# Score products of attention and retention: the product of the low parts over all 128 rows instead of 64

## Chip, cores and metric

The kernel runs on one core of a Trainium2 chip. The metric is the device time of one execution in microseconds (us); the figure for the kernel before is the median of 3 runs.

## What is computed

Four blocks act one after the other on 512 tokens of 1024 channels: twice block 1 (three mixers and a gated feed-forward), twice block 2 (attention, a linear recurrence and a gated MLP). The change touches the scores in two of these parts:

```
# block 1, retention, 4 heads, 64 lanes of q and k per head (written out over all pairs of tokens)
scores = einsum('bhncd,bhnmd->bhncm', qc, kc) * decay        # q, k rotated
# block 2, attention, 8 heads, 128 lanes without and 64 with rotation
q = concatenate([q_nope, q_rope], -1); k = concatenate([k_nope, k_rope], -1)
s = einsum('bqhd,bkhd->bhqk', q, k) * scale
p = softmax(where(mask, s, -1e30))
```

All is float32. The kernel gets there with float32r products (the faster form of TensorE): every operand is split into a high and a low part that sum to it, and a product is hi·hi + hi·lo + lo·hi; the product of the two low parts is left out (`mm3`, lines 319 to 324).

## The kernel before

**Layout.** One program, no loops on the chip: Python writes out some 37,000 instructions, and each engine runs its own in the order in which the program was written. `Stream` (line 147) brings the weights: pieces of 128 x 2048 columns by DMA on the queue of SyncE (SP, line 166), each half ("chunk", 128 x 1024) split into `whi` by ScalarE (line 179) and `wlo` by VectorE (line 180), some four to six chunks ahead of TensorE. `projT` (line 330) multiplies 128 columns of weights with an operand over all 512 tokens: 3 matmuls for each 128 rows, so a chunk is 24 matmuls of 512 columns. There are 8 PSUM buffers, given out in turn.

**Retention** (block 1). After the rotation of q and k, `stack` (line 537) builds for each head, by DMAs between SBUF tiles, `qs` = (q1 hi, q2 hi, q1 lo, q2 lo), 32 lanes each, `ks` = (k1 hi, k2 hi, k1 hi, k2 hi), and `kl` = (k1 lo, k2 lo), the latter in rows 0 to 63 alone (lines 728 to 731). The DMAs of a stack alternate between the queues of GpSimd and SyncE. In `ret_head` (line 609) the scores of 128 keys are two matmuls: line 620 over all 128 rows (hi·hi and hi·lo at once), line 621 over 64 rows (`kl` with the high parts of q). VectorE multiplies them by the decay (line 623). The four heads run in two lanes that step forward between the weight products, so line 620 and line 621 come in groups of two heads: 4 pairs of matmuls, a pause of weight products, 4 pairs again.

**Attention** (block 2, `mla`, line 947). For each head: `scores(h)` (line 986) is, for each of four blocks of 128 queries, five matmuls into one PSUM buffer: lines 997 to 999 the 128 lanes without rotation (q hi·k hi, q hi·k lo, q lo·k hi), line 1000 the rotated lanes (q as hi and lo stacked to 128 rows, the high parts of k held twice), line 1001 the rotated lanes with the low parts of k, over rows 0 to 63. The low parts of k are there in rows 64 to 127 as well (`mla_down` writes the rotated lanes twice). VectorE takes the row maximum (line 1003), ScalarE the exponential (line 1005), VectorE scales (line 1015). Meanwhile TensorE runs the projections of the next head, whose split (lines 314 and 315) ends on VectorE, and what `FILL` lists for this head (products with values, weight products of z_b, the rotated queries of heads 4 to 7 after the scores of head 2). Then `out(h)` (line 1018) transposes the probabilities (line 1026), and the scores of the next head follow.

Of the kernel before, what the change touches and what calls it, by code (L numbers as in the profile page):

```python
# [15 lines left out]
S = 512  # L16
# [12 lines left out]
# column offsets of w_in, block 1  # L29
# [3 lines left out]
# column offsets of w_in, block 2  # L33
# [7 lines left out]
# columns of the per-channel table  # L41
# [16 lines left out]
# rows that are broadcast over the partitions  # L58
# [10 lines left out]
def lru_outside(m):  # L69
    """The channels outside tile m that the gates of tile m depend on: (tile, first, last + 1)."""  # L70
    b0, b1 = (128 * m) // LBW * LBW, ((128 * m + 127) // LBW + 1) * LBW
    out = []
    if b0 < 128 * m:
        out.append((m - 1, b0 - 128 * (m - 1), 128))
    if b1 > 128 * m + 128:
        out.append((m + 1, 0, b1 - 128 * (m + 1)))
    return out
# [7 lines left out]
# the tiles of the recurrence whose gates come with a tile of z_c  # L85
ZPOS = (4, 6, 7, 8)
# what follows the scores of each head: v values, g rotated queries of the second group, p the product
# with the values of the head before, z a z_b
# [44 lines left out]
class Tl:  # L133
    """A tile of 2 KiB per partition, and the slot that it sits in."""
# [12 lines left out]
class Stream:  # L147
    """The weights, in the order in which they are used: pieces of 128 rows, 1024 columns to
    a chunk, two chunks to a DMA; each chunk is split into two float32r parts that sum to it."""
# [19 lines left out]
    def _split(self, c):  # L169
        nc = self.k.nc  # L170
        p = c // 2
        while self.loaded <= p:
            self._load(self.loaded)
            self.loaded += 1
        raw = self.raw[p]
        src = raw[:, 1024 * (c % 2):1024 * (c % 2) + 1024]
        hi = self.k.wp.tile([128, 1024], F32R, tag="whi", name=f"whi{c}")
        lo = self.k.wp.tile([128, 1024], F32R, tag="wlo", name=f"wlo{c}")
        nc.scalar.activation(hi[:], src, AF.Copy)  # L179
        nc.vector.tensor_tensor(lo[:], src, hi[:].bitcast(F32), op=ALU.subtract)  # L180
        self.parts[c] = (hi, lo)
        self.parts.pop(c - RING, None)
        # the next pair is asked for as soon as this one's last half is read
        if c % 2 == 1 and self.total is not None:
            if self.loaded < (self.total + 1) // 2 and self.loaded <= p + RAW:
                self._load(self.loaded)
                self.loaded += 1
# [15 lines left out]
    def take(self, n, spec):  # L203
        """The next n columns of the stream, in two parts."""
        n //= 64
        if self.fill + n > UNITS:
            while self.fill < UNITS:
                self.order.append(None)
                self.fill += 1
            c = self.next()  # L210
            self.fill = 0
            self.cur = c
            if self.total is None:
                self.parts[c] = (Mock(), Mock())
            else:
                assert c <= (self.floor if self.floor is not None else c) + RING - 1
                self.ahead(c if self.lazy else c + AHEAD)
                assert self.split > c
        o = self.fill
        self.order.append((n, spec))  # L220
        for _ in range(n - 1):
            self.order.append(0)
        self.fill += n
        hi, lo = self.parts[self.cur]
        return hi[:, 64 * o:64 * (o + n)], lo[:, 64 * o:64 * (o + n)]
# [5 lines left out]
class Op:  # L231
    """An operand of the tensor engine with features on partitions, in two float32r parts."""
# [5 lines left out]
class Kernel:  # L238
# [64 lines left out]
    def split(self, t, n=512, eng=None):  # L303
        """The two parts of an SBUF tile, which is freed."""
        hi, lo = self.s.t(F32R), self.s.t(F32R)
        self.nc.scalar.activation(hi[:, :n], t[:, :n], AF.Copy)  # L306
        (eng or self.nc.vector).tensor_tensor(lo[:, :n], t[:, :n], hi[:, :n].bitcast(F32), op=ALU.subtract)  # L307
        self.s.f(t)
        return Op(hi, lo)

    def split_ps(self, ps):
        """The two parts of a PSUM tile, which is freed."""
        hi, lo = self.s.t(F32R), self.s.t(F32R)
        self.nc.scalar.activation(hi[:], ps[:], AF.Copy)
        self.nc.vector.tensor_tensor(lo[:], ps[:], hi[:].bitcast(F32), op=ALU.subtract)
        self.p.f(ps)
        return Op(hi, lo)

    def mm3(self, ps, a, b, first, last):
        """ps += a^T b for operands in two parts (the product of the low parts is below float32)."""  # L320
        mm = self.nc.tensor.matmul
        mm(ps, a[0], b[0], start=first, stop=False)  # L322
        mm(ps, a[0], b[1], start=False, stop=False)  # L323
        mm(ps, a[1], b[0], start=False, stop=last)  # L324

# [4 lines left out]
    def projT(self, name, l, cols, op=None, ps=None):  # L330
        """128 columns of a weight matrix times an operand, tokens along the free axis."""
        key = (name, l, cols)
        if key in self.pre:
            return self.pre.pop(key)
        op = op or self.h_op
        bl = self.blocks(name, l, len(op), cols)
        ps = self.p.t()
        for k, w in enumerate(bl):
            self.mm3(ps[:], w, (op[k].hi[:, :], op[k].lo[:, :]), k == 0, k == len(op) - 1)
        return ps  # L340

    def projT_halves(self, specs):
        """The first columns after a norm: the first half of the tokens while the norm of the second
        half is still under way."""
        pend, self.pend = self.pend, None
        ws = self.ws
# [6 lines left out]
        n = len(specs)  # L353
# [32 lines left out]
    def pre_norm(self, tb, g, spill):  # L386
        """h = rmsnorm(x) of a token block."""
        nc = self.nc
        sq = self.small(4, "sq")
        x = [self.x[tb, hf] for hf in range(2)]  # L390
        h = [self.s.t() for hf in range(2)]
# [16 lines left out]
    def transposes(self, tb):  # L408
        """h of a token block to features on partitions, split."""
# [13 lines left out]
    def post_norm(self, tb, ps, g):  # L423
        """x += rmsnorm(y) of a token block, y in PSUM."""
# [19 lines left out]
    def out_proj(self, name, l, nk, get, done, g_post, g_pre, spill, last=False, head=4, tail=4):  # L444
        """y = op @ W with tokens on the partitions, then the norms of each token block as it is done.
        get(k): operand k. done(k): it isn't needed any more."""
# [66 lines left out]
    def norm_tail(self, gn, spill):  # L513
        """What is left of the norms when the next products start."""
        self.transposes(2)
        self.pre_norm(3, gn, spill)
        self.s.f(*gn)
        yield
        self.transposes(3)
        yield  # L520

# [1 line left out]
    def rotate(self, a, b, cos, sin):  # L523
        """The rotated halves of four heads, split: a and b hold them in PSUM, and are freed."""
# [13 lines left out]
    def stack(self, h, parts):  # L538
        """A tile with 32 lanes of head h from each of the parts."""
# [32 lines left out]
    def cf_norm(self, l, c, out):  # L572
        """silu(layernorm(c)), split."""
# [35 lines left out]
    def ret_head(self, h, qs, ks, kl, v, sg, out):  # L609
# [5 lines left out]
        for j in range(NT):  # L615
# [5 lines left out]
            mm(ps[:, :S - n0], kl[h][0:64, js], qs[h][0:64, n0:], start=False, stop=True)  # L621
# [42 lines left out]
    def merge(self, l, wg, cg, wy, ops, acc, n_br, last):  # L664
        """acc (+)= sigmoid(gate) * (op @ W); the last branch gives the operands of the output product."""
# [33 lines left out]
    def tok_proj(self, name, l, cols, n, evac):  # L699
        """Token-major product of h with n columns."""  # L700
# [13 lines left out]
    def mixers1(self, l):  # L714
# [8 lines left out]
        def rope():  # L723
            for nm, a, b in (("q", qa, qb), ("k", ka, kb)):
# [4 lines left out]
                else:  # L729
                    rot["ks"] = [self.stack(h, (x1.hi, x2.hi, x1.hi, x2.hi)) for h in range(4)]  # L730
                    rot["kl"] = [self.stack(h, (x1.lo, x2.lo)) for h in range(4)]
# [71 lines left out]
    def ffn_half(self, l, ch):  # L803
        """A tile of the conv of the up-projection."""
# [53 lines left out]
    def mla_down(self, l):  # L858
        """c_q, c_kv (normed, split) and the rotated key lanes."""
# [20 lines left out]
        for tb in range(NT):  # L880
# [19 lines left out]
            # the rotated key lanes, twice  # L900
# [46 lines left out]
    def mla(self, l, c, zb):  # L947
        """Attention; zb[h] = silu(z_b) becomes y_b of head h."""
# [38 lines left out]
        def scores(h):  # L987
# [4 lines left out]
            for i in range(NT - 1, -1, -1):  # L992
# [8 lines left out]
                mm(ps[:, :nn], qr[0:64, ts], kr.lo[0:64, :nn], start=False, stop=True)  # L1001
# [15 lines left out]
        def out(h):  # L1017
            """The probabilities with keys on partitions: in two parts, those of the last 128 keys whole."""
# [42 lines left out]
        def z(h):  # L1061
            """z_b of a head, whose product may have come first."""
# [37 lines left out]
    def lru(self, l):  # L1100
# [4 lines left out]
        # -8 softplus(-lam), and twice that  # L1105
# [30 lines left out]
        def pack(m):  # L1136
            """The outside channels of tile m in one tile (high, low, high parts), or in one per part."""
# [14 lines left out]
        def gate_weights(m):  # L1152
            """The blocks of tile m, and those of its outside channels."""
# [99 lines left out]
    def gmlp(self, l):  # L1253
# [31 lines left out]
        def spatial(c):  # L1285
            """u * (ws v + bs) * silu(z): z in y."""
# [105 lines left out]
def order():  # L1392
    """The order in which the blocks of the weights are used."""
# [20 lines left out]
def _cols(name, cols):  # L1414
    """Columns of a weight matrix, as a slice or a list."""
# [11 lines left out]
def lay_out(inp):  # L1427
# [19 lines left out]
    def put(key, a):  # L1447
        """a: (taps, channels) -> columns tile by tile, taps inside."""
# [56 lines left out]
```

## Time and profile before

| what | value |
|---|---|
| median of 3 runs | 3267.53 us (3271.23, 3267.14, 3267.53) |
| profiled execution: its span, the only time that the page gives for it | 3272.1 us, 36878 instructions |
| TensorE busy with matmuls | 3216.5 us (98%) |
| TensorE busy with loads of weights | 2651.4 us (81%) |
| VectorE busy | 1871.1 us (57%) |
| ScalarE busy | 1193.4 us (36%) |
| GpSimd busy | 252.0 us (8%) |
| mean rate of the DMA | 103 GB/s |

Matmuls overlap: the busy time of one is longer than the distance from its start to the start of the next. That distance is what a matmul costs on TensorE, so starts are read, not durations. Idle time of an engine that bounds nothing costs nothing.

### The profile page before, as it was taken

The numbers are of one execution on the slowest core, as the hardware profiler recorded it, in microseconds if no ns is written. First come the engines' busy times: TensorE is split into PE (matmuls) and PEld (weight loads), VectorE is DVE, ScalarE is ACT, GpSimd is POOL, SyncE is SP. The second block draws the span as 40 slices with busy tenths as digits, with TensorE's granted clock in tenths as the row PEclk, the third lists the DMA queues.
The fourth block names the chain that finished last, engine by engine and source line by source line (L and its number), as shares of the span: only waits on it lengthen the run. The fifth ranks groups of instructions, "written<-read, shape, count | busy, mean of one in ns | idle before, by whom it ended". The sixth has DMA issues, their size and how long they took to land. (4 is left out here: it accounts for less than half of the span.)

```text
span 3272.1 us, 36878 instructions
## 1 busy us (share of the span) xinstructions
PE 3216.5 (98%) x14808; PEld 2651.4 (81%) x14808; DVE 1871.1 (57%) x2729; ACT 1193.4 (36%) x1798; POOL 252.0 (8%) x354
## 2 busy tenths in 40 slices
PE   8999999999999999999999999999999999999998
PEld 7888888888888888888887887788888788778887
DVE  5677556663667755666358536635445744653543
ACT  4222343342422234334245526522234543642222
POOL 2000010000200001000010002200001000220000
PEclk9999999999999999999999999999999999999999
DMA  5222322332422232233222124322333123333231
GB/s 191 90 92 90 129 88 93 106 113 103 145 84 94 90 129 88 93 107 112 103 103 80 63 95 129 117 103 93 113 116 118 64 77 103 115 117 109 90 103 71
DMA packets 61899, 336.93 MB, mean 103 GB/s; under 512 B 10048, under 2 KB 10176, under 8 KB 26912
## 3 DMA queue, kind: packets, MB, share of 16 engines
q1 hardware_dynamic: 49600, 302.02, 26.3%
q0 software_dynamic: 10976, 30.55, 3.1%
q8 instruction: 116, 1.90, 0.2%
q10 hardware_dynamic: 1152, 2.01, 0.2%
q14 instruction: 55, 0.45, 0.0%
HBM read 310.68 MB, written 8.39 MB: 98 GB/s over the span
## 5 line engine op out<-in xcount | busy, mean ns | idle before, releaser
L322 PE MATMUL p<-hh,whi 128*128 128x512 f32 (+1 forms) x2752 | 1052.4, 382 | 1.6 <-ACT whi L179 1.6
L324 PE MATMUL p<-hh,wlo 128*128 128x512 f32 (+1 forms) x2752 | 1046.7, 380 | 1.4 <-DVE wlo L180 1.4
L323 PE MATMUL p<-hl,whi 128*128 128x512 f32 (+1 forms) x2752 | 1046.8, 380 | 0.0
L180 DVE TENSOR_TENSOR wlo<-raw,whi 128x1024 fp32r<-128x1024 f32 x544 | 676.9, 1252 | 529.4 <-ACT whi L179 528.3
L179 ACT ACTIVATE whi<-raw 128x1024 fp32r<-128x1024 f32 x544 | 562.6, 1052 | 290.6 <-PE p L324 199.4
L322 PEld LDWEIGHTS p<-hh,whi 128*128 128x128 f32 x2752 | 519.9, 189 | 101.3 <-ACT whi L179 2.0
L324 PEld LDWEIGHTS p<-hh,wlo 128*128 128x128 f32 x2752 | 519.4, 189 | 100.7 <-DVE wlo L180 1.7
L323 PEld LDWEIGHTS p<-hl,whi 128*128 128x128 f32 x2752 | 520.0, 189 | 97.1
L322 PE MATMUL p<-s,whi 128*128 128x512 f32 (+1 forms) x768 | 306.8, 399 | 1.7 <-ACT s L306 1.7
L323 PE MATMUL p<-s,whi 128*128 128x512 f32 (+1 forms) x768 | 304.9, 397 | 1.8 <-POOL s L307 1.8
L324 PE MATMUL p<-s,wlo 128*128 128x512 f32 (+1 forms) x768 | 304.9, 397 | 0.0
L323 PE MATMUL p<-wlo,s 128*128 128x512 f32 x640 | 253.8, 397 | 0.0
L322 PE MATMUL p<-whi,s 128*128 128x512 f32 x640 | 253.5, 396 | 0.0
L324 PE MATMUL p<-whi,s 128*128 128x512 f32 x640 | 252.2, 394 | 0.0
L306 ACT ACTIVATE s<-s 128x512 fp32r<-128x512 f32 x168 | 103.2, 626 | 367.4 <-DVE s L688 133.6
L672 ACT ACTIVATE s<-p 128x512 f32<-128x512 f32 x96 | 57.3, 597 | 470.7 <-PE p L324 470.7
L812 DVE SCALAR_TENSOR_TENSOR s<-p,pv,s 128x511 f32<-128x511 f32 (+1 forms) x176 | 131.8, 749 | 122.3 <-ACT s L809 119.2
L683 DVE TENSOR_TENSOR s<-p,s 128x512 f32<-128x512 f32 x96 | 66.3, 691 | 204.0 <-PE p L324 203.9
L566 DVE SCALAR_TENSOR_TENSOR s<-s,pv,s 128x511 f32<-128x511 f32 (+14 forms) x240 | 176.1, 734 | 5.7
L322 PEld LDWEIGHTS p<-s,whi 128*128 128x128 f32 (+1 forms) x768 | 144.6, 188 | 37.5 <-ACT s L306 2.5
L323 PEld LDWEIGHTS p<-s,whi 128*128 128x128 f32 (+1 forms) x768 | 145.0, 189 | 36.6 <-POOL s L307 2.7
L324 PEld LDWEIGHTS p<-s,wlo 128*128 128x128 f32 (+1 forms) x768 | 144.9, 189 | 34.7
(187 smaller groups left out, 3094.3 us busy)
## 6 DMA issues: line engine op xcount, KB each, us to landing
raw<-in_w_dram SPq DMA_DIRECT2D x272, 1024.0 KB, 4.8
s<-in_rows_dram POOLq DMA_DIRECT2D x32, 256.0 KB, 3.5
xd<-s SPq DMA_DIRECT2D x24, 256.0 KB, 2.0
s<-xd POOLq DMA_DIRECT2D x24, 256.0 KB, 3.2
s<-s POOLq DMA_DIRECT2D x88, 64.0 KB, 2.5
s<-s SPq DMA_DIRECT2D x80, 64.0 KB, 2.7
s<-in_cst_dram POOLq DMA_DIRECT2D x16, 256.0 KB, 3.4
s<-in_x_dram POOLq DMA_DIRECT2D x8, 256.0 KB, 4.5
```

The costliest lines, as they stand in the source:

```text
L179: nc.scalar.activation(hi[:], src, AF.Copy)
L180: nc.vector.tensor_tensor(lo[:], src, hi[:].bitcast(F32), op=ALU.subtract)
L306: self.nc.scalar.activation(hi[:, :n], t[:, :n], AF.Copy)
L322: mm(ps, a[0], b[0], start=first, stop=False)
L323: mm(ps, a[0], b[1], start=False, stop=False)
L324: mm(ps, a[1], b[0], start=False, stop=last)
L566: nc.vector.scalar_tensor_tensor(c[:, sh:], glu[:, :S - sh], w(k), c[:, sh:], op0=ALU.mult, op1=ALU.add)
L672: nc.scalar.activation(sgs[m][:], pg[:], AF.Sigmoid)
L683: nc.vector.tensor_tensor(sg[:], py[:], sg[:], op=ALU.mult)
L812: nc.vector.scalar_tensor_tensor(t[:, sh:], ps[:, :S - sh], w(k), t[:, sh:], op0=ALU.mult, op1=ALU.add)
```

## The change

Three places, all in the scores. Line 1001 multiplies all 128 rows of `qr` with all 128 rows of `kr.lo`, line 621 all 128 rows of `kl` with all 128 rows of `qs`, so both now add the product of the low parts. For the latter, line 731 stacks the low parts of k twice, by four DMAs per head instead of two. The number of matmuls, their columns and their order stay. The rest of the diff drops comments and leaves the line numbers.

```diff
@@ ret_head
-            mm(ps[:, :S - n0], kl[h][0:64, js], qs[h][0:64, n0:], start=False, stop=True)
+            mm(ps[:, :S - n0], kl[h][:, js], qs[h][:, n0:], start=False, stop=True)
@@ mixers1, rope
-                    rot["kl"] = [self.stack(h, (x1.lo, x2.lo)) for h in range(4)]
+                    rot["kl"] = [self.stack(h, (x1.lo, x2.lo, x1.lo, x2.lo)) for h in range(4)]
@@ mla, scores
-                mm(ps[:, :nn], qr[0:64, ts], kr.lo[0:64, :nn], start=False, stop=True)
+                mm(ps[:, :nn], qr[:, ts], kr.lo[:, :nn], start=False, stop=True)
```

## Rows read from the trace of the kernel before

**Rows 1.** The page: busy time by engine, and granted clock in 40 slices.
```profile
PE 3216.5 (98%) x14808; PEld 2651.4 (81%) x14808; DVE 1871.1 (57%) x2729; ACT 1193.4 (36%) x1798; POOL 252.0 (8%) x354
PEclk9999999999999999999999999999999999999999
```
**Rows 2.** Groups of instructions by line and shape, TensorE: busy us and mean ns of one.
```profile
L997 PE MATMUL p<-s,s 128*128 128x256 f32 x32 | 12.3, 384 | 0.0
L1001 PE MATMUL p<-s,s 64*128 64x256 f32 x32 | 12.1, 380 | 0.0
...
L1000 PE MATMUL p<-s,s 128*128 128x256 f32 x32 | 8.9, 280 | 0.0
```
**Rows 3.** Timeline, TensorE, scores of head 1, first block 2: start us, duration us, line.
```profile
1747.55 0.40 PE L998 MATMUL p<-s,s 128*128 128x512 f32 x1
...
1748.01 0.40 PE L1000 MATMUL p<-s,s 128*128 128x512 f32 x1
1748.34 0.49 PE L1001 MATMUL p<-s,s 64*128 64x512 f32 x1
1748.76 0.44 PE L997 MATMUL p<-s,s 128*128 128x384 f32 x1
1749.04 0.34 PE L998 MATMUL p<-s,s 128*128 128x384 f32 x1
...
1750.25 0.28 PE L998 MATMUL p<-s,s 128*128 128x256 f32 x1
...
1750.49 0.28 PE L1000 MATMUL p<-s,s 128*128 128x256 f32 x1
...
1752.33 0.40 PE L323 MATMUL p<-s,whi 128*128 128x512 f32 x1
```
**Rows 4.** Timeline, loads of weights (PEld) in the same scores.
```profile
1747.78 0.19 PEld L1000 LDWEIGHTS p<-s,s 128*128 128x128 f32 x1
1748.34 0.18 PEld L1001 LDWEIGHTS p<-s,s 64*128 64x128 f32 x1 [0.37 <-issue]
```
**Rows 5.** Timeline, TensorE, recurrence of block 2: a matmul over 96 rows.
```profile
2003.46 0.39 PE L324 MATMUL p<-s,wlo 128*128 128x512 f32 x1
2003.69 0.39 PE L1170 MATMUL p<-s,whi 96*128 96x512 f32 x1
2003.92 0.39 PE L322 MATMUL p<-s,whi 128*128 128x512 f32 x1
```
**Rows 6.** Timeline, TensorE, retention: two groups of four pairs, each from its start to its end.
```profile
145.71 0.40 PE L620 MATMUL p<-s,s 128*128 128x512 f32 x1
...
149.16 0.40 PE L323 MATMUL p<-hl,whi 128*128 128x512 f32 x1
...
154.45 0.28 PE L620 MATMUL p<-s,s 128*128 128x256 f32 x1
...
157.18 0.40 PE L323 MATMUL p<-hl,whi 128*128 128x512 f32 x1
```
**Rows 7.** Timeline, VectorE and TensorE, from head 2 to the scores of head 4.
```profile
1771.21 0.69 DVE L529 TENSOR_TENSOR s<-p,s 128x512 f32<-128x512 f32 x1 [1.41 <-PE p L324]
...
1779.22 0.69 DVE L1003 TENSOR_REDUCE asm<-p 128x1 f32<-128x512 f32 x1
...
1784.38 1.28 DVE L315 TENSOR_TENSOR s<-p,s 128x512 fp32r<-128x512 f32 x2
...
1785.71 0.50 PE L998 MATMUL p<-s,s 128*128 128x512 f32 x1
```
**Rows 8.** Timeline, VectorE and TensorE, from head 1 to the scores of head 2.
```profile
1755.72 1.41 DVE L315 TENSOR_TENSOR s<-p,s 128x512 fp32r<-128x512 f32 x2
...
1758.74 0.39 PE L998 MATMUL p<-s,s 128*128 128x512 f32 x1
```
**Rows 9.** Timeline, queue of SyncE, ScalarE and VectorE, around the stacks of retention, first layer.
```profile
45.98 13.47 SPq L543 DMA_DIRECT2D s<-s  x20
...
67.34 1.06 ACT L179 ACTIVATE whi<-raw 128x1024 fp32r<-128x1024 f32 x1 [12.30 <-DMA raw<-in_w_dram]
...
80.62 0.69 DVE L553 TENSOR_TENSOR s<-p,s 128x512 f32<-128x512 f32 x1 [1.50 <-PE p L324]
```

## Prediction

> **What bounds the kernel now.** I read the page's busy times first: TensorE is busy for 3216.5 of 3272.1 us, VectorE for 57%, ScalarE for 36% [rows 1]. So TensorE's own sequence sets the time, and a change in it counts in full unless another engine comes into the way just there. The granted clock is full in every slice [rows 1], so nothing is to be had there. But busy is not the same as fast: matmuls overlap, and what one costs is the distance to the next start. So the second view is the groups by line and shape, for matmuls of equal size that differ in length. The products over 64 rows with 256 columns take 380 ns, those on line 1000, of the same columns over 128 rows, 280 ns; and line 997, which follows a product over 64 rows, takes 384 ns although it has 128 rows [rows 2]. Something is lost on either side of each 64-row product. The third view, the timeline of TensorE, tells how much.
>
> **What a 64-row product costs.** In an undisturbed sequence 512 columns take (1748.01 - 1747.55) / 2 = 0.23 us from start to start, and 256 columns (1750.49 - 1750.25) / 2 = 0.12 us [rows 3]; for 384 I take the middle, 0.172. Around line 1001 the starts are: line 1000 at 1748.01, line 1001 at 1748.34, line 997 at 1748.76, line 998 at 1749.04 [rows 3]. These are steps of 0.33, 0.42 and 0.28 us in place of 0.23, 0.23 and 0.172: 1.03 us instead of 0.63, so 0.40 us lost per 64-row product. The loads of weights show where: that of line 1000 starts at 1747.78, one matmul ahead of its use, that of line 1001 at 1748.34, together with its matmul, after 0.37 us of idle time for which no other engine is named [rows 4]. So the load isn't hidden beside the matmul in front when the number of rows changes to 64, and again not when it changes back.
>
> Is it the number of rows, or merely a product with fewer than 128? The recurrence has products over 96 rows between products over 128: starts at 2003.46, 2003.69 and 2003.92, the plain 0.23 us [rows 5]. And is it the end of a sum in PSUM? In these rows line 1170 ends such a sum too, and the next one begins at the usual pace. It is the 64 rows.
>
> **The change on TensorE, part by part.** Lines 1001 and 621 become matmuls of 128 rows with the operands' shapes of lines 1000 and 620, which stand in the trace, so their price needs no guess: the plain pace for their columns. I sum by whole stretches, so that no gap counts twice.
> - Attention, one head: from line 998 of the first block at 1747.55 to the second weight product after the scores at 1752.33 are 4.78 us [rows 3]. At the plain pace: four of 512 columns, five of 384, ten of 256 and one weight product of 512, 0.92 + 0.86 + 1.20 + 0.23 = 3.21 us. Saved 1.57 us per head (four products, 0.39 each). 8 heads x 2 layers: 25.1 us.
> - Retention, a group with two heads' blocks of 512 and 384 columns: 149.16 - 145.71 = 3.45 us [rows 6], plain 4 x 0.23 + 4 x 0.172 + 0.23 = 1.84; saved 1.61. The second group, eight of 256: 157.18 - 154.45 = 2.73 us [rows 6], plain 8 x 0.12 + 0.23 = 1.19; saved 1.54. Two of each in a layer, two layers: 4 x 3.15 = 12.6 us.
> - Gross: 37.7 us for 96 products.
>
> **Where a shorter TensorE meets another engine.** Between two heads of attention TensorE needs what VectorE made of the head before: scaled probabilities for the transposes, and the split low part of the next k for line 998. I looked at this for each head.
> - From head 3 to head 4 there is no slack. VectorE takes the second product of the rotated queries at 1771.21, as soon as TensorE has it, and is then busy almost without a break; it comes to the maximum of head 3's scores only at 1779.22, and the splits of head 4 end at 1784.38 + 1.28 = 1785.66; line 998 of head 4 starts at 1785.71 [rows 7]. This is work of VectorE and ScalarE that doesn't depend on how fast head 3's scores are. So between these points TensorE can't gain: the 1.57 us of head 3 turn into waiting. What heads 0 to 2 saved stays, as the row at 1771.21 waited for TensorE. Loss 2 x 1.57 = 3.1 us.
> - From head 1 to head 2: the splits end at 1755.72 + 1.41 = 1757.13, line 998 starts at 1758.74 [rows 8]. The slack of 1.61 us is just the saving; nothing is lost, or some 0.1 us. All other heads have more filling work, and I book nothing.
> - Retention: VectorE is ahead enough that weight products follow each group; four score buffers of eight are held for a few us longer. I book nothing; if that cover fails, a group loses up to its 1.6 us.
>
> **The added DMAs.** Four more issues per layer on SyncE's queue and as many on GpSimd's. On SyncE 20 of them take 13.47 us [rows 9], 0.67 each, so the weights queued behind come 4 x 0.67 = 2.7 us later. They are split at 67.34 on ScalarE, which waits for them. This is chunk 10, counting the splits from the start. TensorE needs chunk 9 up to 80.62, where VectorE takes its product, and chunk 10 only then [rows 9]. Low part ready some 3 us after 67.34, so over 10 us of cover for 2.7 us: I book nothing, at most 2 x 2.7 = 5.4 us with the cover gone. Behind the stacks on GpSimd's queue stand two decay tables, which nothing needs before the scores of retention at 145.71 [rows 6]; line 621 waits for twice the DMAs there, some 85 us after the last was issued.
>
> **Sum.** 25.1 + 12.6 - 3.1 = 34.6 us. The profiled span would be 3272.1 - 34.6 = 3237.5 us. That span lies 4.6 us over the median of the runs (3267.5); the gaps are TensorE's own and the same in each, so I take the difference from the median: 3232.9 us, 1.06% faster.
>
> **Rivals.**
> - *More of the saving waits for VectorE* (0.08): the slack behind heads 1 and 2 is used up by small delays as well. Three heads in each layer lose all: 37.7 - 6 x 1.57 = 28.3 us, 3239.2 us. For it: the slack of 1.61 us against 1.57 [rows 8]. Against: VectorE's chain moves forward too where it waited for TensorE.
> - *Nothing is lost at head 3* (0.05): 37.7 us, 3229.8 us. It would need a shorter chain on VectorE, and nothing in it is removed.
> - *The stacks delay the weights in full* (0.02): 34.6 - 5.4 = 29.2 us, 3238.3 us. The 10 us of cover speak against it.
> - *It does nothing for the time* (0.03): the gaps are there for another reason than the rows, say the operand that was just stacked or the place of the product in its sum, and 128 rows leave them: 3267.5 us, with a little more work in DMAs. Against it are the products over 96 rows [rows 5], and line 620, which has the stacked operands and 128 rows. The Trainium skill, page "TensorE: Matmul & The Clock Gate", section "Why this matters for your kernels", says that a single matmul over 32 rows takes as long as one over 128; by that rule alone the time would stay. The trace disagrees as soon as 64 and 128 rows alternate: 380 against 280 ns [rows 2].
> - *Slower through the clock* (0.02): the array works over all rows without gaps for 16 passes of scores, and the granted clock falls to its lower level (1.2 instead of 2.4 GHz) there. A pass then takes twice its 3.21 us, 16 x 3.21 = 51 us more: 3232.9 + 51 = 3284 us. It decides the sign once more than 34.6 / 51, about two thirds of the passes, run at the lower level. Against it: weight products of 128 rows without gaps fill most of the span at the full clock [rows 1].
>
> **How the numbers follow.** Forecast 0.80. The range 3227 to 3241 us takes in the forecast, no loss at head 3, more waiting on VectorE and the late weights, with 2 to 3 us for the scatter of the runs (3267.1 to 3271.2). A measurement of this kernel tells about 0.2% (6.5 us) from no change. Faster by more than that: 0.80 + 0.08 + 0.05 + 0.02 = 0.95; same 0.03; slower 0.02.
>
> **What would show it.** Lines 1001 and 621 would have the lengths of lines 1000 and 620 of equal columns (280 ns at 256, some 395 ns at 512), line 997 behind them would lose its 100 ns, and each load of weights would start a matmul ahead. A pass of scores would take 3.2 us in place of 4.8, a group of retention 1.8 and 1.2 in place of 3.4 and 2.7. Between heads 3 and 4 a new wait of TensorE for VectorE of 1.3 to 1.6 us would stand in both layers, and none elsewhere. The forecast is wrong if 128-row products keep the late loads, or if waits for VectorE stand behind several heads.

## The result and the profile after

The changed kernel takes 3235.06 us (median of 4 runs, 3232.47 to 3238.38), the kernel before on the same chip 3267.34 us (4 runs): a ratio of 0.9898, 95% interval 0.9884 to 0.9912, so 1.0% or 32 us less. The forecast was 3232.9 us. The profiled execution has a span of 3236.5 us, 35.6 us under that of before; the forecast was 34.6 us less, so 3237.5 us.

The page first: TensorE's busy time falls by 34.8 us against [rows 1], its share stays at 98%, and the granted clock is 90% of full speed or more in every slice (a digit 9).

```profile
PE 3181.7 (98%) x14808; PEld 2650.7 (82%) x14808; DVE 1867.2 (58%) x2729; ACT 1191.5 (37%) x1798; POOL 255.9 (8%) x362
PEclk9999999999999999999999999999999999999999
```

The groups by line and shape (busy us, mean ns of one). The extra 100 ns on lines 1001 and 997 of [rows 2] are gone:

```profile
L1001 PE MATMUL p<-s,s 128*128 128x256 f32 x32 | 9.0, 282 | 0.0
L997 PE MATMUL p<-s,s 128*128 128x256 f32 x32 | 9.0, 282 | 0.0
```

The timeline (start us, duration us) of TensorE and then of the loads of weights, scores of head 1, which answers to [rows 3, 4]. From line 998 to the second weight product are 1735.43 - 1732.22 = 3.21 us, where there were 4.78, and the load of line 1001 (PEld) now starts at 1732.69, one matmul ahead of its use at 1732.92:

```profile
1732.22 0.40 PE L998 MATMUL p<-s,s 128*128 128x512 f32 x1
...
1732.92 0.39 PE L1001 MATMUL p<-s,s 128*128 128x512 f32 x1
...
1735.43 0.40 PE L323 MATMUL p<-s,whi 128*128 128x512 f32 x1
```
```profile
1732.69 0.19 PEld L1001 LDWEIGHTS p<-s,s 128*128 128x128 f32 x1
```

The same for retention, as in [rows 6]: 148.40 - 146.52 = 1.88 us in place of 3.45, and 154.82 - 153.64 = 1.18 us in place of 2.73.

```profile
146.52 0.39 PE L620 MATMUL p<-s,s 128*128 128x512 f32 x1
...
148.40 0.40 PE L323 MATMUL p<-hl,whi 128*128 128x512 f32 x1
...
153.64 0.28 PE L620 MATMUL p<-s,s 128*128 128x256 f32 x1
...
154.82 0.39 PE L323 MATMUL p<-hl,whi 128*128 128x512 f32 x1
```

From head 2 to head 4 of attention, VectorE and TensorE, in answer to [rows 7]:

```profile
1752.75 0.69 DVE L529 TENSOR_TENSOR s<-p,s 128x512 f32<-128x512 f32 x1 [0.57 <-PE p L324]
...
1760.76 0.69 DVE L1003 TENSOR_REDUCE asm<-p 128x1 f32<-128x512 f32 x1
...
1765.92 1.28 DVE L315 TENSOR_TENSOR s<-p,s 128x512 fp32r<-128x512 f32 x2
```
```profile
1765.36 1.55 PE L1026 MATMUL p<-ident,s 128*128 128x128 f32 x10 [1.20 <-DVE s L1015]
...
1767.26 0.50 PE L998 MATMUL p<-s,s 128*128 128x512 f32 x1
```

VectorE's chain from line 529 to the end of the splits took 1785.66 - 1771.21 = 14.45 us before and takes 1765.92 + 1.28 - 1752.75 = 14.45 us now. TensorE's line 998 of head 4 came 14.50 us after line 529 started on VectorE, and comes 14.51 us after it now. The shorter scores of head 3 gained nothing here: TensorE stops at line 1026 instead.

The waits of TensorE (waited for: us in total, times, longest) have it once in each layer (line 1026). One more wait is new, of 0.6 us at line 323 in the recurrence of the second layer, where the whole kernel had two such waits before; the run with the added DMAs alone has three as well, so it doesn't need the new products:

```profile
PE p L323 <- POOL s L307: 2.4, 3, 0.9
PE p L1026 <- DVE s L1015: 2.4, 2, 1.2
...
PE p L926 <- ACT s L877: 0.6, 1, 0.6
```

The same lines in the kernel before; it has none at line 1026:

```profile
PE p L926 <- ACT s L877: 4.9, 2, 2.9
PE p L323 <- POOL s L307: 1.8, 2, 0.9
```

The wait at line 926 doesn't need the shorter scores to fall from 4.9 us: with the added DMAs alone, and all products as before, it is 0.5 us.

### The profile page after: what moved, and what is told of

It reads as the page before. It is cut to its first block, busy times and chain, and to the rows that moved or that the text cites. A ratio compares the mean times of both kernels' runs of the same rounds, so it can differ in the third digit from the quotient of the medians.

```text
span 3236.5 us, 36908 instructions
## 1 busy us (share of the span) xinstructions
PE 3181.7 (98%) x14808; PEld 2650.7 (82%) x14808; DVE 1867.2 (58%) x2729; ACT 1191.5 (37%) x1798; POOL 255.9 (8%) x362
```

## Experiments

The theory under test: each place where TensorE goes from 128 to 64 rows and back costs about 0.39 us, and the loads of weights there don't run ahead; it isn't the product's own work, nor its operands, nor the DMAs. And behind head 3 VectorE sets the time. Ratios are to runs of the kernel before on the same chip.

### Attention alone

```diff
-                mm(ps[:, :nn], qr[0:64, ts], kr.lo[0:64, :nn], start=False, stop=True)
+                mm(ps[:, :nn], qr[:, ts], kr.lo[:, :nn], start=False, stop=True)
```

> The kernel before with line 1001 alone over 128 rows; retention stays as it was (line 621 over 64 rows, low parts of k stacked once). Theory (a change between 64 and 128 rows exposes a load of weights, 0.39 us per product, and head 3 can't use its share): 64 products x 0.39 = 25.1 us less 2 to 3 us of new waits for VectorE behind head 3, so some 22 to 23 us under the kernel before, about 3245 us. If the operand made by stacking DMAs were the cause, attention (where q is stacked and the low part of k is not) and retention would not share one price per product.

Measured: 3249.9 us against 3270.24, ratio 0.9938 (0.9921 to 0.9955), 20.3 us less (interval 15 to 26) for the 22 to 23 expected; the new wait behind head 3 is there with the same 2.4 us. The groups by line and shape show each half of the change for itself: line 1001 at its plain length, line 621 still 100 ns longer.

```profile
L1001 PE MATMUL p<-s,s 128*128 128x256 f32 x32 | 9.0, 282 | 0.0
L621 PE MATMUL p<-s,s 64*128 64x256 f32 x16 | 6.1, 380 | 0.0
```

### Retention alone, and its DMAs alone

```diff
-                    rot["kl"] = [self.stack(h, (x1.lo, x2.lo)) for h in range(4)]
+                    rot["kl"] = [self.stack(h, (x1.lo, x2.lo, x1.lo, x2.lo)) for h in range(4)]
@@ in the first of the two kernels alone
-            mm(ps[:, :S - n0], kl[h][0:64, js], qs[h][0:64, n0:], start=False, stop=True)
+            mm(ps[:, :S - n0], kl[h][:, js], qs[h][:, n0:], start=False, stop=True)
```

> The kernel before with line 621 alone over 128 rows and the low parts of k stacked twice; attention stays. Theory: 32 products x 0.39 = 12.6 us under the kernel before, about 3255 us, with no new wait of TensorE. If the added DMAs cost what they take on SyncE's queue, 12.6 - 5.4 = 7.2 us. attn_only and ret_only together should give the whole difference of the change (some 32 to 36 us).

> The kernel before with the low parts of k stacked twice, and all products over 64 rows as before: the DMAs of the change without its products. Theory (over 10 us of cover for weights that come 2.7 us later): no difference from the kernel before, 3267 us. Rival, DMAs not hidden: up to 5.4 us more, 3273 us. Rival, the gaps come from the half-filled operand and not from the rows: 12.6 us less, 3255 us.

Measured: retention alone 3256.38 us against 3270.24, ratio 0.9963 (0.9948 to 0.9977), 13.9 us less for the 12.6 expected. The two halves add up to 34.2 us. The DMAs alone: 3271.37 us, ratio 1.0004 (0.9995 to 1.0013), so no difference, and neither the late weights nor the half-filled operand is a cause.

### 96 rows

```diff
-                mm(ps[:, :nn], qr[:, ts], kr.lo[:, :nn], start=False, stop=True)
+                mm(ps[:, :nn], qr[0:96, ts], kr.lo[0:96, :nn], start=False, stop=True)
-            mm(ps[:, :S - n0], kl[h][:, js], qs[h][:, n0:], start=False, stop=True)
+            mm(ps[:, :S - n0], kl[h][0:96, js], qs[h][0:96, n0:], start=False, stop=True)
```

> The changed kernel with lines 1001 and 621 over rows 0 to 95 in place of all 128, which leaves out a part of the low-times-low product. Theory (only products that fit in 64 rows make TensorE change over): as fast as the changed kernel, 3235 us, and every load of lines 1001 and 621 one matmul ahead. Rival, any product under 128 rows pays: as slow as before, 3267 us. Rival, the price goes with the rows left out: half way, 3251 us.

Measured: 3235.35 us, ratio 0.9894 (0.9879 to 0.9909), the same as the changed kernel. Lined up with the changed kernel, the score products start at the same distances. Groups by line and shape:

```profile
L1001 PE MATMUL p<-s,s 96*128 96x256 f32 x32 | 9.0, 283 | 0.0
```

So it is not "fewer than 128 rows". 96 rows cost what 128 cost; 64 between 128 cost 0.39 us more. The Trainium skill, page "TensorEngine Tiling (Array Packing)", sections "Tiling Modes" and "Key Properties", offers a reason: the array can be set to 128, 64 or 32 rows, and a change of that mode drains the engine. The measurements agree as far as they go: 96 rows, which fit neither 64 nor 32, cost nothing, and going from 128 to 64 rows and back has a price, 0.40 us. That the engine drains there is not shown by any trace here.

### The 64-row products together

Both kernels put the four low products of a head behind the other sixteen of that head; they differ in the rows of line 1001. Lines are shifted here: that product is line 1007, and line 1001 is what was line 1000.

```diff
+                pss[i] = ps
+            for i in range(NT - 1, -1, -1):
...
+                mm(pss[i][:, :nn], qr[0:64, ts], kr.lo[0:64, :nn], start=False, stop=True)   # grouped64
+                mm(pss[i][:, :nn], qr[:, ts], kr.lo[:, :nn], start=False, stop=True)         # grouped128
```

> The changed kernel with another order in the scores of attention: lines 997 to 1000 for all four blocks of queries first, then the four products of line 1001, over 128 rows. The control for grouped64. TensorE's work is the same; the first row maximum starts some 2 us later, so waits for VectorE grow behind heads 1 and 3. Theory: 3 to 8 us over the changed kernel, all of it as waits of TensorE for VectorE between heads.

> As grouped128, but line 1001 over rows 0 to 63 (as in the kernel before), so that the four 64-row products of a head stand together: one change of rows before them and one behind, instead of four of each. Theory (the change of rows costs, not the product): 16 heads x 0.39 = 6.3 us over grouped128, or less where TensorE waits for VectorE anyway; inside the run of four the loads start a matmul ahead again and 256 columns take 0.12 us. Rival (each 64-row product is slow by itself): 64 x 0.39 = 25 us over grouped128.

Measured: 3234.98 us with 128 rows, ratio 0.9898 (0.9884 to 0.9913), and 3240.19 us with 64, ratio 0.9913 (0.9897 to 0.9930). The difference of the medians, 5.2 us, is near the 6.3 of one change per head and far from the 25 of a price per product, but the intervals of the ratios overlap. So the timeline decides (head 1, 64 rows):

```profile
1734.14 0.28 PE L1001 MATMUL p<-s,s 128*128 128x256 f32 x1
1734.35 0.92 PE L1007 MATMUL p<-s,s 64*128 64x512 f32 x4
...
1735.53 0.40 PE L323 MATMUL p<-s,whi 128*128 128x512 f32 x1
```

From the last 128-row score product to the second weight product behind are 1.39 us. At the plain pace of the forecast, 0.12 + (0.23 + 0.172 + 0.12 + 0.12) + 0.23 = 0.99 us. So four 64-row products in a row cost 0.40 us together, as much as one did alone. With the starts of both traces lined up, each of the 16 heads is 0.36 to 0.41 us longer with 64 rows than with 128, 6.2 us in all. Within the run a 64-row product has its plain length (groups by line and shape):

```profile
L1007 PE MATMUL p<-s,s 64*128 64x256 f32 x32 | 6.5, 281 | 0.0
```

The expectation for the control was wrong: the later maxima cost nothing. TensorE's wait for the scaled probabilities didn't grow, it is 1.4 us in both layers together, where the changed kernel has 2.4, and from head to head the starts are as far apart as there, to 0.03 us. Head 3's maxima weren't waiting for its scores in the first place: from line 998 of head 3 to that of head 4 (999 in the grouped kernels) are 11.58 us with 64 and with 128 rows, as in the changed kernel.

### Without the low products

```diff
-                mm(ps[:, :nn], qr[:, ts], kr.lo[:, :nn], start=False, stop=True)
-            mm(ps[:, :S - n0], kl[h][:, js], qs[h][:, n0:], start=False, stop=True)
```

> The changed kernel without lines 1001 and 621: the products with the low parts of k are left out, their stacks stay. It measures what such a product costs at the plain pace. Theory: 16 x 0.64 in attention + 8 x 0.64 in retention = 15.4 us, less 1.3 us which head 3 can't use, 14 us under the changed kernel, 3221 us. Together with the gaps, 64-row products then had cost 3267 - 3221 = 46 us, of which two thirds were not their own work. Rival (the product lies beside other work): no difference from the changed kernel.

Measured: 3221.37 us (3219.48 to 3221.94), ratio 0.9856 (0.9841 to 0.9871), where 3221 were expected: 13.7 us under the changed kernel. A product at the plain pace is not hidden. The starts show the price better than the medians: the groups of retention are 0.83 and 0.48 us shorter than in the changed kernel, where the columns of the products left out make 0.80 and 0.48.

### More DMAs in front of the weights

```diff
+        junk = self.tc.dram_tile((24 * 32, 512), F32, name=f"junk{l}")
...
+                    for i in range(24):
+                        nc.sync.dma_start(junk[32 * i:32 * i + 32, :], x2.lo[32 * (i % 4):32 * (i % 4) + 32, :].bitcast(F32))
```

> The changed kernel with 24 more DMAs per layer of block 1 on SyncE's queue, behind the stacks of k (32 rows of the low part of the second half each, to a scratch tensor in HBM that nothing reads). The weights queued behind come 24 x 0.66 = 15.8 us later. Theory (cover of 10.4 us: chunk 10 is split by 71.0 us and needed at 81.4 us in the changed kernel): 5.4 us of new waiting of TensorE per layer, some 11 us in all, 3246 us. Rival, the queue has no cover: 31.6 us. Rival, the queue never matters: 0.

Measured: 3242.34 us (3239.70 to 3244.48), ratio 0.9921 (0.9906 to 0.9935). First SyncE's queue, then TensorE, in the first layer:

```profile
61.63 12.39 SPq L734 DMA_DIRECT2D junk<-s  x24
```
```profile
80.86 0.50 PE L322 MATMUL p<-hh,whi 128*128 128x512 f32 x1 [0.70 <-ACT whi L179]
...
82.12 0.50 PE L324 MATMUL p<-hh,wlo 128*128 128x512 f32 x1 [0.53 <-DVE wlo L180]
```

TensorE waits for chunk 10 for the first time, 1.2 us here and 1.4 us in the other layer; lined up with the changed kernel, its starts fall behind by 1.6 and 1.7 us. The mechanism is the expected one, the size is not: the 24 issues took 12.39 us (0.52 each, not 0.66), so they went past the cover of 10.4 us by 2.0 us instead of 5.4. In the changed kernel the issues of the stacks take 15.81 us, where they took 13.47 [rows 9]:

```profile
46.79 15.81 SPq L543 DMA_DIRECT2D s<-s  x24
```

So it is shown that the cover is more than the 2.3 us of the change and less than 12.4 us. The medians differ by more than the waits account for (the ratios 0.9921 and 0.9898 are some 7 us apart); that part stays open.

### Can head 3's share be had as well?

The changed kernel again as reference, then one split of weights moved from in front of head 3's maxima to head 2, then also the scaling of line 877 moved ahead of a split on ScalarE.

```diff
-            self.ws.ahead(self.ws.cur + AHEAD + 1)
+            self.ws.ahead(self.ws.cur + AHEAD + (2 if h == 2 else 1))
@@ mla_down, in the last kernel alone
+        scale(NT - 1)
+
         def trans():
-            scale(NT - 1)
             yield
```

> The changed kernel once more, as the reference for the two that follow, on one chip with them: 3235 us, some 34 us under the kernel before.

> The changed kernel with one split of weights moved: before the scores of head 2 one chunk more is split ahead, so that the split that stands on VectorE in front of head 3's row maxima (1.2 us) is done a head earlier. Theory (VectorE's chain from the rotated queries to the splits of head 4 is what TensorE waits for behind head 3): the chain is 1.2 us shorter and the wait of TensorE for the scaled probabilities, 1.2 us in each layer, is gone or nearly so; some 2.4 us under the changed kernel in all, 3233 us, too little for the median to tell, so the waits decide. Rival (the wait hangs on something else, say the exponentials on ScalarE): the wait stays at 1.2 us.

> split_early, and the scaling of the last block of c_q and c_kv (lines 877 and 878) moved ahead of the next split of weights on ScalarE's queue. Theory (the scaling stands behind a split that waits for its weights to land, and TensorE's transposes on line 926 wait for the scaling: 2.0 and 2.9 us in the kernel before, 0.6 us in one layer of the changed one, by when the DMA lands): these waits go to zero, 0 to 5 us less, and less scatter from run to run; 3230 to 3233 us. Rival (the scaling comes late because GpSimd's reciprocal root comes late): the wait stays.

Measured: 3237.76 us (3236.71 to 3239.84) for the reference, 3232.88 (3231.30 to 3234.07) and 3232.13 us (3231.48 to 3232.91) for the two. The waits of the reference:

```profile
PE p L926 <- ACT s L877: 2.4, 2, 2.2
PE p L1026 <- DVE s L1015: 2.4, 2, 1.2
```

With the split moved no wait at line 1026 is left, and with the scaling moved none at line 926 either; the waits of split_early still have the latter:

```profile
PE p L926 <- ACT s L877: 0.7, 2, 0.4
```

So it is VectorE's chain that ate head 3's share. But the moved split gets back less than half of it. TensorE, then VectorE, with the split moved, from head 3 to head 4, and a wait that is new:

```profile
1752.61 0.39 PE L998 MATMUL p<-s,s 128*128 128x512 f32 x1
...
1763.55 0.50 PE L998 MATMUL p<-s,s 128*128 128x512 f32 x1
```
```profile
1762.21 1.28 DVE L315 TENSOR_TENSOR s<-p,s 128x512 fp32r<-128x512 f32 x2
```
```profile
PE p L997 <- DVE s L1050: 0.4, 2, 0.2
```

From line 998 of head 3 to that of head 4 are 1763.55 - 1752.61 = 10.94 us, where the reference, the changed kernel and the kernel before all have 11.58 or 11.59, in both layers. That is 0.64 us of head 3's 1.53. VectorE still sets the time: its splits end at 1762.21 + 1.28 = 1763.49, just ahead of line 998, and it now makes TensorE wait at line 997 inside head 3's scores as well.

All runs of either kernel lie under all of the reference; the medians are 4.9 and 5.6 us lower, of which head 3 makes up 1.3 and 1.4 us and line 926 up to 2.4. But the intervals of the ratios (0.9890 to 0.9919, 0.9872 to 0.9905, 0.9872 to 0.9901) overlap, so what is shown is that the waits at lines 1026 and 926 are gone, not by how much the time falls.

## Why the prediction was right

- **The price of a 64-row product** came from starts, not from busy times, and held: 1.57 us booked per head, 4.78 - 3.21 = 1.57 measured; groups of retention 1.61 and 1.54 booked, 1.57 and 1.55 measured. With the starts of the same matmuls in both traces lined up, the 16 heads give 24.6 us (25.1 booked), and retention 12.5 us (12.6 booked).
- **The cause** was read from the products over 96 rows [rows 5] and the late load [rows 4]. The runs with 96 rows and with the 64-row products together confirm that the change of rows costs; the rival that the change does nothing fell with the first result. The rule of the Trainium skill cited there (page "TensorE: Matmul & The Clock Gate", section "Why this matters for your kernels") is about 32 rows, of which no run here has a product; for 64 rows the like holds inside a run of such products, 281 against 282 ns, and fails at its ends.
- **Head 3** lost its share, as booked: lined up in the same way, it gains its 1.5 us in the scores and has given back 1.53 us in layer 1 and 1.52 us in layer 2 by line 998 behind it (1.57 booked). The wait that the profile names is smaller, 1.2 us: it counts from the end of the matmul in front, while the next could have started before that end. So the wait is shorter than the 1.3 to 1.6 us that the prediction named as a sign. Behind head 1 nothing was lost, but that was close: 0.04 us of slack was left by the numbers, and 1741.84 - (1740.40 + 1.28) = 0.16 us is what the changed kernel has. Of what head 1 saved, VectorE's chain behind it moved along by only 0.12 us.

```profile
1740.40 1.28 DVE L315 TENSOR_TENSOR s<-p,s 128x512 fp32r<-128x512 f32 x2
```
```profile
1741.84 0.40 PE L998 MATMUL p<-s,s 128*128 128x512 f32 x1
```

- **The DMAs** cost nothing that the runs can tell, as booked: 1.0004 (0.9995 to 1.0013) with them alone.
- **What the sum left out**: 34.6 us booked and 35.6 us between the spans agree partly by luck. Lined up, the 35.6 us are 24.6 + 12.5 of the scores, less 3.05 behind the two heads 3, plus 4.3 at line 926, less some 2.8 that were lost elsewhere; neither of the last two was booked. The waits at line 926 went from 4.9 to 0.6 us. They depend on when a piece of weights lands: ScalarE's scaling (line 877) stands behind a split (line 179) that waits for it, in the first layer 6.79 us before and 4.81 us now:

```profile
1708.28 1.06 ACT L179 ACTIVATE whi<-raw 128x1024 fp32r<-128x1024 f32 x1 [6.79 <-DMA raw<-in_w_dram]
```
```profile
1694.48 1.06 ACT L179 ACTIVATE whi<-raw 128x1024 fp32r<-128x1024 f32 x1 [4.81 <-DMA raw<-in_w_dram]
```

The same program has 2.4 us of the waits at line 926 in another execution. On the other side the clock took some back. It is at its lower level (1.2 of 2.4 GHz) in short stretches, which are not the same in each execution; the row of slices [rows 1], which the prediction read as a full clock throughout, hides them, as a digit stands for a mean over 82 us. Below are weight products at the end of the recurrence of block 2, first layer: changed kernel, then the kernel before (length; busy us and counts of TensorE, its loads, VectorE, ScalarE, GpSimd; granted clock as a share of full speed; share and rate of DMA).

```profile
2080.00:2084.00 4.00, 4.00 (x14) 3.15 (x13) 3.76 (x6) 2.30 (x3) 0.51 (x1) 0.69 1.15 281
```
```profile
2106.00:2110.00 4.00, 4.00 (x20) 3.30 (x19) 3.65 (x4) 1.09 (x2) 0.54 (x1) 1.00 1.03 310
```

Here 14 matmuls take the time of 20, at a mean clock of 0.69 against 1.00; TensorE had waited for the recurrence shortly before in both. Both effects are a few us, about as much as the runs of one kernel differ (3232.47 to 3238.38). The prediction had put "2 to 3 us for the scatter" into the range without naming these two sources.

The rival of a slower kernel through the clock has nothing for it: the scores run at the full pace, 3.21 us for head 1 and at most 3.35 us for any (4.87 before).

## What to carry to other kernels

Read the cost of a matmul from start to start, and look at its neighbours: a product over 64 rows among products over 128 cost 0.4 us here that its own columns don't explain, and filling the rows, here with a term that the sum of products leaves out otherwise, removed it. If the rows can't be filled, put such products together: four in a row cost as much as one. Before booking a gain on the bounding engine in full, look at each place where it picks up another engine's result and ask whether that chain began before or after the part that gets shorter; the one place here where it began before kept its whole share. Starts lined up in two traces tell such shares to 0.1 us, where the medians of a few runs tell some us.

## What was not expected of the hardware

96 rows cost no more than 128 (283 and 282 ns at 256 columns), 64 rows in a run no more either (281 ns); the whole price, 0.40 us, lies in going over and back once. And DMAs of 64 KB from SBUF to HBM were issued every 0.52 us on SyncE's queue (24 in 12.39 us), those between SBUF tiles every 0.66 us (24 in 15.81 us).
